# A two-layer decoder trunk on one core: a layer's last output products by column halves, and the pre-norm's second sum of squares on VectorE

## The chip, the cores and the metric

The kernel is one program on one core of a Trainium2 chip. The metric is device time in microseconds (us) from the first to the last work of one execution; every number is for that one core. The engines are TensorE (PE: matrix products and transposes, with PEld for its weight loads), VectorE (DVE), ScalarE (ACT), GpSimd (POOL), and SyncE (SP), whose queue starts all the DMA transfers. Each engine takes its instructions in a fixed order and waits on semaphores for the others.

## The reference

256 positions of 1024 channels go through two layers. Each layer has a token mixer (layer 0: native sparse attention; layer 1: a Mamba-2 scan) and then a gated ConvFFN. Each of these four sub-layers is wrapped in two norms:

```
def rms_norm(x, gain):
    y = xf * lax.rsqrt(jnp.mean(xf * xf, axis=-1, keepdims=True) + RMS_EPS)
    return (y * gain.astype(jnp.float32)).astype(x.dtype)
...
        hn = rms_norm(h, gains[0])
...
        h = h + rms_norm(m, gains[1])
        f = conv_ffn(rms_norm(h, gains[2]), ffn_w_up[i], ffn_conv_w[i], ffn_conv_b[i], ffn_w_down[i])
        h = h + rms_norm(f, gains[3])
```

So between two sub-layers the output of the first is normed and added to `h` (the post-norm), and the new `h` is normed for the next sub-layer (the pre-norm). Nothing in the next sub-layer can start before that.

## The kernel before

The stream `h` lies in SBUF as two tiles, `h0` and `h1`, of 128 positions by 1024 channels each; they are called token blocks 0 and 1 here. Every product is done in three passes (`mm3`), since both operands are split into a high and a low part: high by high, low by high, high by low. Weights come by DMA in pieces of 512 KB (`raw`); ACT casts each to its high part (`whi`, line 56), and DVE subtracts to get the low part (`wlo`, line 57). These two run all through the program, and the buffers of `raw`, `whi` and `wlo` are reused in turn (five of each in the common pool): a cast waits until PE has done with an older piece, and a load waits until DVE has done with an older `raw`.

A sub-layer ends in `out_mm`. It has a list of jobs (one for each 128 rows of the contraction) and two PSUM accumulators, one for each column half of 512 channels. It loops over the jobs and, inside, over the two halves. For the ConvFFN of layer 0 the last call has five jobs (the hidden pairs 17 to 21, whose `hm` tiles come from ACT and DVE), for that of layer 1 four; for the attention four; in the scan layer each group of heads is one call of four jobs. The call for token block 0 stands before that for token block 1.

Then, for each block, comes `after`: the post-norm (`postnorm`: ACT sums the squares of both halves, `junk` on line 126; POOL adds, `ms` on line 117, and takes the power -0.5, `rstd` on line 119; DVE multiplies by the gain, `fg` on line 161, and by `rstd` and adds to `h`, line 164), and the pre-norm (`prenorm_steps`: the same sum of squares on `h` through `rms`, then `xn` on DVE, line 146, eight transposes `pt` on PE, line 65, and the split into `xhi` on ACT and `xlo` on DVE). After the last sub-layer the post-norm alone follows, and then the stores. In the scan layer DVE first scales the accumulators into a tile `osb` (lines 812 and 814), and the post-norm reads that.

The order of instructions on each engine is not that of the source: a scheduler lays it out when the program is built, from its own estimates of when each result will be there. So a change in one place also moves other instructions nearby. The ConvFFN, the attention and the scan start their first product with token block 0 alone (`pv`), so that block 1's norm can run beside it.

Of the kernel before, what the change touches and what calls it, by code (L numbers as in the profile page):

```python
# [10 lines left out]
BF16 = mybir.dt.bfloat16  # L11
AF = mybir.ActivationFunctionType
OP = mybir.AluOpType
# [7 lines left out]
EPS = 1e-6  # L21
# [12 lines left out]
def trunk(ctx, tc, x, gains, consts, masks, params, nsa_in, nsa_vw, cmp_w1, nsa_out,  # L34
          ssd_in, ssd_dt, ssd_out, ffn_up, ffn_down, out):
    nc = tc.nc
# [3 lines left out]
    sp = ctx.enter_context(tc.tile_pool(name="sp", bufs=2))  # L40
# [8 lines left out]
    def tiny(shape, name):  # L49
        return sp.tile(shape, F32, name=name, tag="tiny", bufs=16)  # L50
# [16 lines left out]

    last_mm = [None]

    # weights: load, then split into two exact float32r parts; pieces of 4 KB a partition  # L70
    class Weights:
        def __init__(self, src, a, b, pool=None, n=5, order=(), first=nc.scalar.copy, into=None, lows=()):
            self.m, self.parts = min(a, 1024 // b), []
# [19 lines left out]
    weights = Weights  # L93
# [7 lines left out]
    mhalf = cp.tile([128, 1], F32, name="mhalf")  # L101
# [13 lines left out]
    def rstd_of(a, b, n):  # L115
        ms = tiny([128, n], "ms")
        nc.gpsimd.tensor_scalar(ms, a, b, EPS, op0=OP.mult if isinstance(b, float) else OP.add, op1=OP.add)  # L117
        r = tiny([128, n], "rstd")
        nc.gpsimd.tensor_tensor(r, ms, mhalf.to_broadcast([128, n]), op=OP.pow)
        return r  # L120

    def rms(src):
        ss = tiny([128, 2], "ss")
        for c in range(2):
            junk = sp.tile([128, 512], BF16, name="junk", tag="junk", bufs=2)
            nc.scalar.activation(junk, src[c], AF.Square, scale=1.0 / 32, accum_out=ss[:, c:c + 1])  # L126
        return rstd_of(ss[:, 0:1], ss[:, 1:2], 1)

    def new_xt():
        return (cp.tile([128, 2, KT, 128], F32R, name="xhi"), cp.tile([128, 2, KT, 128], F32R, name="xlo"))  # L130
# [8 lines left out]
        return marks  # L139

    def prenorm_steps(i, g, xt, pins):
        r = rms([h[i][:, :512], h[i][:, 512:]])
        xn = sp.tile([128, D], F32, name="xn", tag="xn", bufs=2)
        for c in range(2):
            cs = slice(512 * c, 512 * c + 512)
            z = nc.vector.scalar_tensor_tensor(xn[:, cs], h[i][:, cs], r, g[:, cs], op0=OP.mult, op1=OP.mult)
        yield [z.ins]
        for c in range(2):
            pt = pa([128, 4, 128], "pt")
            with after_ins(pins[c]):  # L150
                for k in range(4):
                    tr(pt[:, k, :], xn[:, 512 * c + 128 * k:512 * c + 128 * k + 128], ident)
            o = (slice(None), i, slice(4 * c, 4 * c + 4))
            yield [split(xt[0][o], xt[1][o], pt)]
# [11 lines left out]
    def mm3(o, ahi, alo, bhi, blo, first, last):  # L166
        mm(o, ahi, bhi, start=first, stop=False)
        mm(o, ahi, blo, start=False, stop=False)
        return mm(o, alo, bhi, start=False, stop=last)
# [41 lines left out]
    def out_mm(acc, i, jobs, first, last):  # L211
        marks = []
        ts = slice(128 * i, 128 * i + 128)
        for n, (a, ka, w, kw) in enumerate(jobs):
            for c in range(2):
                cs = slice(512 * c, 512 * c + 512)
                marks.append(mm3(acc[c], a[0][:, ka, ts], a[1][:, ka, ts], *w(kw, cs), first and n == 0,
                                 last and n == len(jobs) - 1).ins)
        return marks

    # ---------------------------------------------------------------- NSA
    def nsa(np_, xt, after):
        def one(shape, name, dt=F32):
            return np_.tile(shape, dt, name=name, bufs=1)
# [283 lines left out]
        after(0, accs[0], marks[-FN:][:2])  # L508
        after(1, accs[1])

    # ---------------------------------------------------------------- ConvFFN
    silu = [None]

    def tap0(c, ps, base, nt):
# [46 lines left out]
        after(0, accs[0], marks[-FA:][:2])  # L561
        after(1, accs[1])

    # ---------------------------------------------------------------- SSD
    def ssd(zp, yp, xt):
        def one(shape, name, dt=F32):
            return zp.tile(shape, dt, name=name, bufs=1)
# [248 lines left out]
                    after(i, [osb[:, i, :512], osb[:, i, 512:]], (None, None))  # L816
            todo = []

    # ---------------------------------------------------------------- trunk
    xt = new_xt()  # L820
    gain0 = load_gain(0)
    scaled, *marks0 = prenorm(0, gain0, xt)
# [161 lines left out]
```

## Time and profile before

| | |
|---|---|
| time before, median of 3 runs | 758.35 us (757.01 to 758.54) |
| span of the profiled execution, first to last instruction | 755.2 us (its own time is not given apart; the span lies 3.15 us under the median) |
| TensorE busy | 732.1 us (97% of the span) |
| VectorE busy | 570.3 us (76%) |
| ScalarE busy | 468.7 us (62%) |
| GpSimd busy | 65.6 us (9%) |

A busy share is an average over the program. With PE at 97%, what counts is where PE stands still (about 23 us in all, 6 of them after its last product), and which engine it waits for there.

### The profile page before, as it was taken

Reading aid. Unit: us, or ns where it says so; the run is one execution under the profiler, and the core shown is the slowest. Engines: PE = TensorE matmul, PEld = TensorE weight load, DVE = VectorE, ACT = ScalarE, POOL = GpSimd, SP = SyncE. Lnnn points to the kernel's source line nnn. Section 1 sums busy time; section 2 is a strip of 40 time slices with the busy share of each in tenths; the row PEclk is TensorE's granted clock in tenths of the full one; section 3 lists DMA queues with packets and bytes.
Section 4 is the critical chain, followed back from the end, with each engine's and each line's share of the span. In section 5 each row is a group of like instructions: output and inputs, shape, how many; then the busy total and the mean of one; then the engine's idle time right before and its main releaser. Section 6 shows DMA issues by size and latency. Waiting matters only on the chain.

```text
span 755.2 us, 13761 instructions
## 1 busy us (share of the span) xinstructions
PE 732.1 (97%) x5300; PEld 666.9 (88%) x5300; DVE 570.3 (76%) x927; ACT 468.7 (62%) x885; POOL 65.6 (9%) x95
## 2 busy tenths in 40 slices
PE   6989999999999999999999999999999999999996
PEld 4989877679999999997899998898778999999995
DVE  4687987747977767777698877679887967776783
ACT  5576768646655555565776686666566656555651
POOL 2310121211000000000000000024220000000000
PEclk9999999999999999999999999999999999999999
DMA  8864440315656555665355564125644665666531
GB/s 310 287 229 146 149 139 1 113 56 176 209 179 199 192 189 177 204 209 178 120 174 183 168 223 136 61 84 157 212 156 148 210 190 183 186 201 195 172 112 57
DMA packets 35427, 125.96 MB, mean 167 GB/s; under 512 B 4064, under 2 KB 4384, under 8 KB 35360
## 3 DMA queue, kind: packets, MB, share of 16 engines
q1 hardware_dynamic: 35360, 125.07, 51.1%
q8 instruction: 42, 0.69, 0.4%
q14 instruction: 25, 0.20, 0.1%
HBM read 124.00 MB, written 1.05 MB: 166 GB/s over the span
## 4 chain that ended last, share of the span: by engine, by line
PE 80%; DVE 9%; ACT 4%; DMA 3%; issue 2%; POOL 1%; SPq 0%; DVEq 0%; POOLq 0%; ACTq 0%
PE pu L61 44%; PE acc L61 18%; PE pv L61 5%; DVE wlo L57 4%; PE pt L65 3%; PE po L61 3%; PE sa L61 1%; ACT junk L126 1%; PE py L61 1%; ACT whi L56 1%; PE sb L61 1%; DMA gain<-in_gains 1%; PE pcx L61 1%; PE pc L61 1%; DMA raw<-in_ffn_down 1%
## 5 line engine op out<-in xcount | busy, mean ns | idle before, releaser
L57 DVE TENSOR_TENSOR wlo<-raw,whi 128x1024 fp32r<-128x1024 f32 (+1 forms) x220 | 268.3, 1226 | 81.1 <-ACT whi L56 80.5
L56 ACT CAST whi<-raw 128x1024 fp32r<-128x1024 f32 x223 | 231.1, 1045 | 106.9 <-PE pu L61 58.1
L61 PE MATMUL pu<-xhi,whi 128*128 128x256 f32 x1056 | 297.1, 281 | 0.1
L61 PE MATMUL pu<-xhi,wlo 128*128 128x256 f32 x1056 | 295.9, 281 | 0.0
L61 PE MATMUL pu<-xlo,whi 128*128 128x256 f32 x1056 | 295.4, 280 | 0.0
L61 PEld LDWEIGHTS pu<-xhi,whi 128*128 128x128 f32 x1056 | 199.1, 189 | 2.3 <-issue 0.5
L61 PEld LDWEIGHTS pu<-xlo,whi 128*128 128x128 f32 x1056 | 199.2, 189 | 1.2
L61 PEld LDWEIGHTS pu<-xhi,wlo 128*128 128x128 f32 x1056 | 199.0, 189 | 0.3 <-issue 0.2
L521 DVE SCALAR_TENSOR_TENSOR cc<-pu,pr,cc 128x255 f32<-128x255 f32 (+2 forms) x248 | 111.3, 477 | 6.8 <-ACT cc L515 3.7
L61 PE MATMUL acc<-whi,hm 128*128 128x512 f32 x352 | 114.6, 391 | 0.6 <-ACT hm L56 0.6
L61 PEld LDWEIGHTS acc<-whi,hm 128*128 128x128 f32 x352 | 66.1, 188 | 14.2 <-ACT hm L56 1.0
L61 PE MATMUL acc<-wlo,hm 128*128 128x512 f32 x176 | 69.0, 392 | 0.0
L515 ACT ACTIVATE cc<-pu,pr 128x256 f32<-128x256 f32 x112 | 57.8, 558 | 9.0 <-PE pu L61 8.8
L56 ACT CAST hm<-cc 128x256 fp32r<-128x256 f32 x44 | 17.8, 404 | 45.5 <-DVE cc L549 45.5
L117 POOL TENSOR_SCALAR ms<-ss 128x1 f32<-128x1 f32 x16 | 7.7, 479 | 420.5 <-ACT junk L126 420.5
L61 PE MATMUL acc<-whi,gw 128*128 128x512 f32 x128 | 41.3, 398 | 0.0
L61 PEld LDWEIGHTS acc<-wlo,hm 128*128 128x128 f32 x176 | 33.0, 188 | 5.6
L61 PE MATMUL pv<-whi,xhi 128*128 128x256 f32 (+1 forms) x128 | 36.4, 295 | 1.0 <-ACT whi L56 0.6
L61 PE MATMUL pv<-whi,xlo 128*128 128x256 f32 (+1 forms) x128 | 34.9, 288 | 1.0 <-DVE xlo L57 0.9
L61 PE MATMUL pv<-wlo,xhi 128*128 128x256 f32 (+1 forms) x128 | 35.2, 285 | 0.2 <-DVE wlo L57 0.2
L57 DVE TENSOR_TENSOR hm<-cc,hm 128x256 fp32r<-128x256 f32 x44 | 18.6, 423 | 14.6 <-ACT hm L56 14.6
L61 PEld LDWEIGHTS acc<-whi,gw 128*128 128x128 f32 x128 | 24.0, 188 | 5.2
(211 smaller groups left out, 896.4 us busy)
## 6 DMA issues: line engine op xcount, KB each, us to landing
raw<-in_ffn_up SPq DMA_DIRECT2D x88, 512.0 KB, 4.5
raw<-in_ffn_down SPq DMA_DIRECT2D x44, 512.0 KB, 4.7
raw<-in_ssd_in SPq DMA_DIRECT2D x40, 512.0 KB, 4.7
raw<-in_nsa_in SPq DMA_DIRECT2D x18, 512.0 KB, 5.0
raw<-in_ssd_out SPq DMA_DIRECT2D x16, 512.0 KB, 4.0
gain<-in_gains SPq DMA_DIRECT2D x8, 512.0 KB, 4.6
raw<-in_cmp_w SPq DMA_DIRECT2D x8, 512.0 KB, 5.4
raw<-in_nsa_out SPq DMA_DIRECT2D x8, 512.0 KB, 4.5
```

The costliest lines, as they stand in the source:

```text
L56: r = copy(hi, src)
L57: eng.tensor_tensor(lo, src, hi.bitcast(F32), op=OP.subtract)
L61: last_mm[0] = nc.tensor.matmul(*a, **k)
L65: last_mm[0] = nc.tensor.transpose(*a)
L117: nc.gpsimd.tensor_scalar(ms, a, b, EPS, op0=OP.mult if isinstance(b, float) else OP.add, op1=OP.add)
L126: nc.scalar.activation(junk, src[c], AF.Square, scale=1.0 / 32, accum_out=ss[:, c:c + 1])
L515: nc.scalar.activation(c, ps, AF.Identity, bias=pr[:, base + nt:base + nt + 1], scale=pr[:, base + nt - 1:base + nt])
L521: nc.vector.scalar_tensor_tensor(c[:, s:], ps[:, :S - s], wv, c[:, s:], op0=OP.mult, op1=OP.add)
```

## The change

It has two parts. In `out_mm`, a call that is the last one for its accumulators (`last`) now goes through all jobs for the first column half and then through all jobs for the second. In the pre-norm, `rms` is replaced by `rms_two`: ACT sums the squares of the first half only; POOL adds the epsilon to that sum; DVE multiplies the second half by itself and accumulates on top of POOL's result; POOL takes the power. The post-norm keeps `rms`. (Two comment lines are also gone.)

```
+    def square(src, out):
+        junk = sp.tile([128, 512], BF16, name="junk", tag="junk", bufs=2)
+        nc.scalar.activation(junk, src, AF.Square, scale=1.0 / 32, accum_out=out)
+
     def rms(src):
         ss = tiny([128, 2], "ss")
         for c in range(2):
-            junk = sp.tile([128, 512], BF16, name="junk", tag="junk", bufs=2)
-            nc.scalar.activation(junk, src[c], AF.Square, scale=1.0 / 32, accum_out=ss[:, c:c + 1])
+            square(src[c], ss[:, c:c + 1])
         return rstd_of(ss[:, 0:1], ss[:, 1:2], 1)
+
+    def rms_two(src):
+        ss, part = tiny([128, 2], "ss"), tiny([128, 1], "part")
+        square(src[0], ss[:, 0:1])
+        nc.gpsimd.tensor_scalar(part, ss[:, 0:1], EPS, None, op0=OP.add)
+        junk = sp.tile([128, 512], BF16, name="junk", tag="junk", bufs=2)
+        nc.vector.tensor_tensor_reduce(junk, src[1], src[1], 1.0 / 1024, part, OP.mult, OP.add, ss[:, 1:2])
+        r = tiny([128, 1], "rstd")
+        nc.gpsimd.tensor_tensor(r, ss[:, 1:2], mhalf, op=OP.pow)
+        return r
...
     def prenorm_steps(i, g, xt, pins):
-        r = rms([h[i][:, :512], h[i][:, 512:]])
+        r = rms_two([h[i][:, :512], h[i][:, 512:]])
...
     def out_mm(acc, i, jobs, first, last):
         marks = []
         ts = slice(128 * i, 128 * i + 128)
-        for n, (a, ka, w, kw) in enumerate(jobs):
-            for c in range(2):
-                cs = slice(512 * c, 512 * c + 512)
-                marks.append(mm3(acc[c], a[0][:, ka, ts], a[1][:, ka, ts], *w(kw, cs), first and n == 0,
-                                 last and n == len(jobs) - 1).ins)
+        steps = [(n, c) for n in range(len(jobs)) for c in range(2)]
+        if last:
+            steps.sort(key=lambda z: z[1])
+        for n, c in steps:
+            a, ka, w, kw = jobs[n]
+            cs = slice(512 * c, 512 * c + 512)
+            marks.append(mm3(acc[c], a[0][:, ka, ts], a[1][:, ka, ts], *w(kw, cs), first and n == 0,
+                             last and n == len(jobs) - 1).ins)
         return marks
```

In the built program the new sum is two instructions on DVE, both listed as `ISA`: the product with its accumulation, and a read of the accumulator into `ss`. There are eight of each, two for every sub-layer's pre-norm. Three places show how the order moved.

**TensorE, end of layer 0's ConvFFN, token block 0.** `acc_2519` and `acc_2520` are its two column halves; `hm_3600`, `hm_3697`, `hm_3782`, `hm_3879` and `hm_3964` are the hidden pairs 17 to 21. The run of 30 products begins with `hm_3600`. Before, the twelve that end the run:

```order
L61 MATMUL acc_2519<-whi_4005,hm_3879 128x512
L61 MATMUL acc_2519<-wlo_4006,hm_3879 128x512
L61 MATMUL acc_2519<-whi_4005,hm_3879 128x512
L61 MATMUL acc_2520<-whi_4005,hm_3879 128x512
L61 MATMUL acc_2520<-wlo_4006,hm_3879 128x512
L61 MATMUL acc_2520<-whi_4005,hm_3879 128x512
L61 MATMUL acc_2519<-whi_4011,hm_3964 128x512
L61 MATMUL acc_2519<-wlo_4012,hm_3964 128x512
L61 MATMUL acc_2519<-whi_4011,hm_3964 128x512
L61 MATMUL acc_2520<-whi_4011,hm_3964 128x512
L61 MATMUL acc_2520<-wlo_4012,hm_3964 128x512
L61 MATMUL acc_2520<-whi_4011,hm_3964 128x512
```

After, these are products 10 to 21 of the run:

```order
L61 MATMUL acc_2519<-whi_4005,hm_3879 128x512
L61 MATMUL acc_2519<-wlo_4006,hm_3879 128x512
L61 MATMUL acc_2519<-whi_4005,hm_3879 128x512
L61 MATMUL acc_2520<-whi_3975,hm_3600 128x512
L61 MATMUL acc_2520<-wlo_3976,hm_3600 128x512
L61 MATMUL acc_2520<-whi_3975,hm_3600 128x512
L61 MATMUL acc_2520<-whi_3993,hm_3697 128x512
L61 MATMUL acc_2519<-whi_4011,hm_3964 128x512
L61 MATMUL acc_2519<-wlo_4012,hm_3964 128x512
L61 MATMUL acc_2519<-whi_4011,hm_3964 128x512
L61 MATMUL acc_2520<-wlo_3994,hm_3697 128x512
L61 MATMUL acc_2520<-whi_3993,hm_3697 128x512
```

The first product with the last pair, `hm_3964`, stood behind 24 others and now stands behind 16; the scheduler put four products of the second half in front of it.

**VectorE, from layer 0's ConvFFN into the scan layer.** `acc_2521` and `acc_2522` are the halves of token block 1, `xlo` the split input of the next sub-layer for block 0, `wlo_4413` a piece of the scan's weights. Before:

```order
L164 SCALAR_TENSOR_TENSOR h0_70<-fg_4079,rstd_4087,h0_70 128x512 x2
L57 TENSOR_TENSOR wlo_4413<-raw_4410,whi_4412 128x1024
L146 SCALAR_TENSOR_TENSOR xn_4102<-h0_70,rstd_4100,gain_4077 128x512 x2
L161 TENSOR_TENSOR fg_4119<-acc_2521,gain_4075 128x512
L161 TENSOR_TENSOR fg_4119<-acc_2522,gain_4075 128x512
L57 TENSOR_TENSOR xlo_2031<-pt_4105,xhi_2030 128x512
L57 TENSOR_TENSOR xlo_2031<-pt_4112,xhi_2030 128x512
L164 SCALAR_TENSOR_TENSOR h1_71<-fg_4119,rstd_4127,h1_71 128x512 x2
```

After:

```order
L177 SCALAR_TENSOR_TENSOR h0_70<-fg_4079,rstd_4087,h0_70 128x512 x2
L137 ISA junk_4098,ss_4093<-h0_70,part_4094 128x512
L137 ISA ss_4093 128x1
L159 SCALAR_TENSOR_TENSOR xn_4102<-h0_70,rstd_4100,gain_4077 128x512 x2
L174 TENSOR_TENSOR fg_4119<-acc_2521,gain_4075 128x512
L57 TENSOR_TENSOR wlo_4413<-raw_4410,whi_4412 128x1024
L174 TENSOR_TENSOR fg_4119<-acc_2522,gain_4075 128x512
L57 TENSOR_TENSOR xlo_2031<-pt_4105,xhi_2030 128x512
L57 TENSOR_TENSOR xlo_2031<-pt_4112,xhi_2030 128x512
L177 SCALAR_TENSOR_TENSOR h1_71<-fg_4119,rstd_4127,h1_71 128x512 x2
```

The weight's `wlo_4413` stood ahead of block 0's `xn`; it now stands between the two `fg` of block 1, ahead of both `xlo`.

**VectorE, from the scan layer into layer 1's ConvFFN, token block 1.** `acc_6489` and `acc_6490` are the halves of block 1's last accumulators; `wlo_6563`, `wlo_6569` and `wlo_6731` are pieces of the ConvFFN's weights, the first two those of its second `pv`. Before:

```order
L57 TENSOR_TENSOR wlo_6563<-raw_6560,whi_6562 128x1024
L57 TENSOR_TENSOR xlo_4147<-pt_6454,xhi_4146 128x512
L57 TENSOR_TENSOR wlo_6569<-raw_6566,whi_6568 128x1024
L814 SCALAR_TENSOR_TENSOR osb_6052<-acc_6489,rstd_6413,osb_6052 128x512
L814 SCALAR_TENSOR_TENSOR osb_6052<-acc_6490,rstd_6413,osb_6052 128x512
L161 TENSOR_TENSOR fg_6517<-osb_6052,gain_6417 128x512 x2
L164 SCALAR_TENSOR_TENSOR h1_71<-fg_6517,rstd_6525,h1_71 128x512 x2
L57 TENSOR_TENSOR wlo_6731<-raw_6728,whi_6730 128x1024
L146 SCALAR_TENSOR_TENSOR xn_6540<-h1_71,rstd_6538,gain_6419 128x512 x2
```

After:

```order
L174 TENSOR_TENSOR fg_6517<-osb_6052,gain_6417 128x512
L830 SCALAR_TENSOR_TENSOR osb_6052<-acc_6490,rstd_6413,osb_6052 128x512
L57 TENSOR_TENSOR wlo_6563<-raw_6560,whi_6562 128x1024
L174 TENSOR_TENSOR fg_6517<-osb_6052,gain_6417 128x512
L177 SCALAR_TENSOR_TENSOR h1_71<-fg_6517,rstd_6525,h1_71 128x512 x2
L57 TENSOR_TENSOR wlo_6569<-raw_6566,whi_6568 128x1024
L137 ISA junk_6536,ss_6531<-h1_71,part_6532 128x512
L137 ISA ss_6531 128x1
L57 TENSOR_TENSOR wlo_6731<-raw_6728,whi_6730 128x1024
L159 SCALAR_TENSOR_TENSOR xn_6540<-h1_71,rstd_6538,gain_6419 128x512 x2
```

`wlo_6569` moved from the front of block 1's post-norm to behind its `h1`, ahead of the new sum, and `wlo_6731` now stands between the new sum and the `xn` that needs POOL's power of it.

## Rows read from the trace of the kernel before

**Rows 1.** The page's head: span, then busy time of each engine.

```profile
span 755.2 us, 13761 instructions
...
PE 732.1 (97%) x5300; PEld 666.9 (88%) x5300; DVE 570.3 (76%) x927; ACT 468.7 (62%) x885; POOL 65.6 (9%) x95
```

**Rows 2.** The tile `xn`: ns minimum/median/maximum; who waited, us and times.

```profile
L146 DVE SCALAR_TENSOR_TENSOR xn<-h,rstd,gain x16: 743/749/753, 9.4 to 568.2; 128x512 f32<-128x512 f32 x16
...
PE pt L65: 7.5, 5
```

**Rows 3.** The line 126, squares of one half: the square, the accumulator's read.

```profile
L126 ACT ACTIVATE junk<-h x16: 615/631/632, 3.8 to 565.6; 128x512 bf16<-128x512 f32 x16
L126 ACT ACTIVATION_READ_ACCUMULATOR junk<-h x16: 185/187/189, 4.4 to 566.2; 128x1 f32 x16
```

**Rows 4.** Timeline, end of layer 0's ConvFFN: start, us, instruction, idle before.

```profile
340.88 0.39 PE L61 MATMUL acc<-whi,hm 128*128 128x512 f32 x1
...
348.84 0.39 PE L61 MATMUL acc<-whi,hm 128*128 128x512 f32 x1
349.39 0.40 ACT L56 CAST hm<-cc 128x256 fp32r<-128x256 f32 x1 [1.82 <-DVE cc L549]
349.85 0.50 PE L61 MATMUL acc<-whi,hm 128*128 128x512 f32 x1 [0.62 <-ACT hm L56]
...
352.90 1.06 ACT L56 CAST whi<-raw 128x1024 fp32r<-128x1024 f32 x1 [0.67 <-PE acc L61]
```

**Rows 5.** Timeline, from layer 0's ConvFFN into the scan layer.

```profile
358.46 1.35 DVE L161 TENSOR_TENSOR fg<-acc,gain 128x512 f32<-128x512 f32 x2 [0.35 <-ACT junk L126]
359.73 1.28 DVE L57 TENSOR_TENSOR xlo<-pt,xhi 128x512 fp32r<-128x512 f32 x2
...
360.46 0.39 PE L61 MATMUL pv<-whi,xlo 128*128 128x256 f32 x1
```

**Rows 6.** Timeline, attention into ConvFFN, token block 0's pre-norm.

```profile
165.30 0.63 ACT L126 ACTIVATE junk<-h 128x512 bf16<-128x512 f32 x1 [1.92 <-DVE h L164]
...
166.78 0.30 POOL L117 TENSOR_SCALAR ms<-ss 128x1 f32<-128x1 f32 x1 [2.37 <-ACT junk L126]
...
167.17 0.56 POOL L119 TENSOR_TENSOR rstd<-ms,mhalf 128x1 f32<-128x1 f32 x1
...
168.67 1.29 PE L65 MATMUL pt<-ident,xn 128*128 128x128 f32 x8 [0.58 <-DVE xn L146]
```

**Rows 7.** Timeline, the same place, token block 1.

```profile
172.63 1.40 DVE L164 SCALAR_TENSOR_TENSOR h<-fg,rstd,h 128x512 f32<-128x512 f32 x2
...
173.95 1.22 DVE L57 TENSOR_TENSOR wlo<-raw,whi 128x1024 fp32r<-128x1024 f32 x1
...
176.91 1.29 PE L65 MATMUL pt<-ident,xn 128*128 128x128 f32 x8
```

**Rows 8.** Timeline of VectorE and of GpSimd, out of the scan layer.

```profile
551.49 2.35 DVE L57 TENSOR_TENSOR wlo<-raw,whi 128x1024 fp32r<-128x1024 f32 x2
...
552.54 1.39 POOL L117 TENSOR_SCALAR ms<-ss 128x1 f32<-128x1 f32 x1 [2.42 <-ACT junk L126]
```

**Rows 9.** Timeline, out of the scan layer: TensorE's two waits, block 1's `h`.

```profile
555.51 0.63 PE L65 MATMUL pt<-ident,xn 128*128 128x128 f32 x4 [1.48 <-DVE xn L146]
...
564.17 1.41 DVE L164 SCALAR_TENSOR_TENSOR h<-fg,rstd,h 128x512 f32<-128x512 f32 x2 [0.84 <-POOL rstd L119]
...
568.37 0.66 PE L65 MATMUL pt<-ident,xn 128*128 128x128 f32 x4 [1.53 <-DVE xn L146]
```

**Rows 10.** Waits of ScalarE, 505 to 562 us: total, times, longest.

```profile
ACT whi L56 <- PE acc L61: 1.8, 5, 0.4
```

**Rows 11.** Timeline, start of the program, token block 1's transposes.

```profile
16.93 0.63 PE L65 MATMUL pt<-ident,xn 128*128 128x128 f32 x4 [0.65 <-DVE xn L146]
```

**Rows 12.** Timeline, the last product and the last square.

```profile
748.51 0.39 PE L61 MATMUL acc<-whi,hm 128*128 128x512 f32 x1
...
748.99 0.60 ACT L126 ACTIVATE junk<-acc 128x512 bf16<-128x512 f32 x1
```

## The prediction

> **What bounds the kernel now.** The page comes first: PE is busy in 97% of the span [rows 1]. So an edit counts only where PE stands still, or comes to. The view of the tile `xn` says who makes it stand at the norms: 7.5 us in 5 waits for `xn` [rows 2]. Then the timeline of each passage between two sub-layers is read for what ends the wait. Out of the attention PE waits 0.58 us for block 0 and nothing for block 1 [rows 6, 7]; out of the scan it waits 1.48 and 1.53 us [rows 9]; at the start 0.65 us [rows 11]. Out of layer 0's ConvFFN it waits before the norm, 0.62 us for the last `hm` [rows 4].
>
> **What the change costs, part by part.**
>
> *The column halves and the squares.* One could expect the first half's square to move under the second half's products, and a square to vanish from the path. The end of the program shows that it was under them already: PE starts the last product at 748.51 and ends it at 748.90, and ACT starts the second half's square at 748.99 [rows 12]. Three products, the lead that a half has in the old order, last 0.68 us; a square of 0.63 [rows 3] fits in that. What is left to gain is the 0.09 us between the two, say 0.05. The end term is -0.05.
>
> *The last `hm`.* The new order asks for each job's operands earlier. In rows 4 thirty-six products start from 340.88 to 348.84, the last 24 of them being the first 24 of the run: (348.84 - 340.88)/35 = 0.227 us each. The run thus begins at 340.88 + 12 x 0.227 = 343.61, and the first product with `hm_3964` was due at 349.07; it started at 349.85, since ACT began that `hm` at 349.39 [rows 4]. The built order puts it behind 16 products instead of 24, so PE is there at 343.61 + 16 x 0.227 = 347.25. ACT and DVE get `hm` ready by work that the change does not touch, so PE stands for 2.60 us instead of 0.78: **+1.82**, eight products that used to cover the wait. They follow after it, when nothing waits for them. It is zero only if `hm` comes 1.8 us earlier; nothing can make it more, since behind 349.85 the two orders have the same products.
>
> *A weight ahead of `xlo`.* The cast at 352.90 waited for PE to give back a piece of down weights [rows 4]. That is the piece of pair 17; its last use was the sixth product of block 1's run and is now the eighteenth. The cast and its `wlo` slide, and the built order has the `wlo` between the two `fg`, ahead of `xlo`. Before, DVE waited 0.35 us ahead of the first `fg`, did two `fg` and two `xlo`, and PE took the first `xlo` at 360.46, 0.05 after its end [rows 5]. A `wlo` takes 1.22 [rows 7]. DVE, no longer idle, saves about 0.25 of it; `xlo` and with it PE comes 0.97 later. Bounds 0 (it slips in earlier) and 1.2. I take **+0.95**. The new sums here cost nothing: block 0's `xn` is ready about 0.5 us before PE has finished block 1's run; if that cover went, 0.3 us would show.
>
> *The new sum, by itself.* The old path from the first square to the power is 167.17 - 165.30 = 1.87 us [rows 6]. The new one is: square and read 0.69 (two of them and a hop of 0.1 take 166.78 - 165.30 = 1.48), a hop of 0.1 to POOL, 0.30 there, 0.04 to DVE, the sum, its read, a hop of 0.1. No row shows the new instruction. From below it is a square's step of 0.63; the nearest row is `xn`, DVE's other operation on 512 fp32 elements with two SBUF tensors, at 0.75 [rows 2]; from above it is 1.28, `xn` plus another 512 elements at a cycle each (2 x 0.64, a pair's span of 1.28 in rows 5). For its read I take ACT's 0.19 [rows 3]. The sum is 0.69 + 0.1 + 0.30 + 0.04 + 0.75 + 0.19 + 0.1 = 2.17, so each pre-norm is **0.3 longer**, not shorter, with bounds 0.2 and 0.85. The second square gone from ACT buys nothing: ACT is busy 62% [rows 1].
>
> [...]
>
> *The new sum in its queues.* It also makes DVE and POOL wait for each other, and POOL waits for DVE's `wlo`: `ms`, normally 0.30 [rows 6], took 1.39 while two `wlo` ran from 551.49 to 553.84, and ended 0.09 behind them [rows 8]. [...] The old path gave POOL two operations in a row; the new one has DVE between them, and the scheduler has put a `wlo` into the gap in places.
> - Attention into ConvFFN: block 0's transposes are 0.3 later. Block 1's `h` follows at about 173.0 and the `wlo` behind it, shifted with it, ends at 175.55 [rows 7]. POOL's first operation waits for it, to 175.75; sum and read to 176.7; the power to 177.4; `xn` 0.75 more; transposes at 178.3 instead of 176.91 [rows 7], where PE did not wait before. **+1.4** in all (bounds 0.3, if only block 0's part shows, and 2.4, with two sums of 1.28).
> - Out of the scan, block 0's wait falls from 1.48 to about 0.75, for the built order puts eight more products in front of its transposes (8 x 0.23 = 1.9 against an `xn` that is 0.3 to 1.2 later). Block 1's `h` can so start at 563.25 instead of 564.17 [rows 9]. But `wlo_6569` now stands behind it, 564.55 to 565.75. The sum follows until 566.95; `wlo_6731` until 568.1, with POOL's power locked out; 0.56 for the power [rows 6], 0.75 for `xn`. Transposes at 569.5 instead of 568.37 [rows 9]: **+1.2** (bounds -1.1, the first wait's gain kept and more, and +2.3). The second `pv` needs `wlo_6569` as well, and its stall lies inside this.
> - Start: the same pattern, a `wlo` between the sum and `xn` of block 1. Its wait of 0.65 [rows 11] grows to about 1.2: **+0.55** (0 to 1.1).
>
> In the scan's output phase the four jobs' weights are wanted earlier as well, but the scheduler interleaves the halves there, and each `wlo` comes as PE reaches it; zero, with 0.5 either way.
>
> **The sum**: -0.05 + 1.82 + 0.95 + 1.4 + 1.2 + 0.55 = +5.9 us on the span of 755.2. The span lies 3.15 under the median of the runs; on the median it gives 758.35 + 5.9 = **764.2 us**. With all lower bounds together (`hm` stays) it is 758.35 + 1.0 = 759.3, with all upper ones and the 0.5 of the output phase 767.7.
>
> **The rivals.**
> - *Sums at double length.* The 1.28 for 0.75 adds 0.53 wherever a sum is exposed: at the start, twice out of the attention, once into the scan, twice out of it. 6 x 0.53 = 3.2 more: 767.4 us. [...]
> - *The output phase of the scan takes up the lateness.* If DVE's casts and scalings from 505 to 562 us ran at their own pace, PE's lateness of 4.7 by then would eat into the waits of 1.48 and 1.53 and the scan would end as before, less what the halves give: accumulators that are half done 2 us earlier, and both waits gone. That is faster: 758.35 - 3.0 = 755.3 us at the best. It decides where DVE's chain there does not wait for PE. Against it: ACT's casts in that stretch waited for PE five times [rows 10], and DVE's `wlo` wait for those casts, so the lateness is handed on.
> - *Half of that*, the lateness eaten by the waits but no gain left: 4.7 - 3.0 = 1.7 of lateness, less than 1 us of which the halves return: 758.5 to 759.5 us, no change.
> - *The change does not do what it says.* Where the scheduler interleaves the halves again, as in the built order of the scan's middle groups, the halves are as before and only the sums remain: 0.55 + 1.4 + 1.2 = 3.2, 761.5 us. For the ConvFFN the built order excludes it; this lies inside the forecast's range.
>
> **How the numbers follow.** A measurement of this kernel can tell about 0.2%, 1.5 us. Forecast, 759.9 to 767: 0.60, its likeliest 764.2. Doubled sums, 767 and above: 0.12. No change, 756.8 to 759.9: 0.15. Faster: 0.13. The range leaves out most of the faster case and the end of the slow one: 757 to 768. Slower by over 0.2% is 0.60 + 0.12 = 0.72.
>
> **What the changed profile would show.** PE's wait for the last `hm` of layer 0 near 2.4 us (right) or 0.6 (wrong). `xlo` into the scan behind a `wlo` and PE waiting about 1 us for it. The new sum on DVE at 0.75 and its read near 0.2. POOL's operations of the pre-norm over 1 us wherever a `wlo` runs. Out of the scan a first wait under 1 us and a second above 1.5 us, or a stall in the second `pv` ahead of it. The end: the last square 0.04 instead of 0.09 behind the last product. What would make the prediction wrong is above all an earlier `hm`, or a scan whose end does not feel that its start was late.

## The result, and the profile after

The changed kernel takes 762.55 us (median of 4 runs, 760.3 to 763.11) against 757.68 for the kernel before (4 runs, 755.85 to 758.54): ratio 1.0066, 95% interval 1.0051 to 1.0081. It is slower by 5.0 us where 5.9 was forecast; 764.2 was too much by 1.7, and 0.7 of that is the kernel before, whose median fell from 758.35 to 757.68 with the fourth run. The profiled execution, the fastest of the four (760.3), has a span of 758.5 us, 1.8 under its time. With the same difference the profiled execution of before, whose span is 755.2, took about 757.0. The two spans differ by 3.3 us; the rest of the 5.0 is taken up with the halves alone, below.

The page's head shows PE as busy as before, and the time as added standing [rows 1]:

```profile
span 758.5 us, 13752 instructions
...
PE 731.8 (96%) x5300; PEld 665.9 (88%) x5300; DVE 575.8 (76%) x943; ACT 463.8 (61%) x869; POOL 66.8 (9%) x95
```

The new sum in the views of the tiles `part` and `ss` (ns minimum/median/maximum). The sum takes 752 ns, what `xn` takes (749 [rows 2]), not twice that, and its read 84, half of ACT's 187 [rows 3]. POOL's two operations have maxima of 1.10 and 1.47 us beside medians of 0.22 and 0.57; below it is seen where.

```profile
L135 POOL TENSOR_SCALAR part<-ss x8: 221/222/1101, 4.8 to 567.5; 128x1 f32<-128x1 f32 x8
L137 DVE CUSTOM_DVE_ANT_0 junk<-h,part x8: 749/752/753, 5.1 to 568.5; 128x512 bf16<-128x512 f32 x8
```

```profile
L137 DVE DVE_READ_ACCUMULATOR2_ANT ss<- x8: 82/84/86, 5.7 to 569.2; 128x1 f32 x8
L139 POOL TENSOR_TENSOR rstd<-ss,mhalf x8: 559/566/1471, 5.9 to 569.4; 128x1 f32<-128x1 f32 x8
```

The timeline at the end of layer 0's ConvFFN answers to [rows 4]. `hm` is ready 0.3 us earlier than before, as is the whole program there, but PE wants it eight products sooner and stands for 2.48 us instead of 0.62:

```profile
343.44 1.05 ACT L56 CAST whi<-raw 128x1024 fp32r<-128x1024 f32 x1 [0.54 <-PE acc L61]
344.40 1.01 ACT L531 ACTIVATE cc<-pu,pr 128x256 f32<-128x256 f32 x2
...
349.07 0.41 ACT L56 CAST hm<-cc 128x256 fp32r<-128x256 f32 x1 [1.90 <-DVE cc L565]
349.53 0.50 PE L61 MATMUL acc<-whi,hm 128*128 128x512 f32 x1 [2.48 <-ACT hm L56]
```

Into the scan [rows 5], a `wlo` stands between the two `fg`, `xlo` starts 2.13 us later, and PE waits 0.77 us for it, where rows 5 list no wait:

```profile
359.52 0.68 DVE L174 TENSOR_TENSOR fg<-acc,gain 128x512 f32<-128x512 f32 x1
...
360.12 1.21 DVE L57 TENSOR_TENSOR wlo<-raw,whi 128x1024 fp32r<-128x1024 f32 x1
...
361.86 1.28 DVE L57 TENSOR_TENSOR xlo<-pt,xhi 128x512 fp32r<-128x512 f32 x2
362.59 0.39 PE L61 MATMUL pv<-whi,xlo 128*128 128x256 f32 x1 [0.77 <-DVE xlo L57]
```

Out of the attention [rows 6, 7]. Block 0's transposes come 1.11 us earlier than before and block 1's only 0.39, so this passage costs 0.72. In block 0 VectorE has finished `h` at 163.30 + 1.42 = 164.72 and then waits 0.51 us for POOL's `part` before it starts its sum. In block 1 `part` takes 0.97 and ends at 174.15, 0.09 behind the `wlo`:

```profile
163.30 1.42 DVE L177 SCALAR_TENSOR_TENSOR h<-fg,rstd,h 128x512 f32<-128x512 f32 x2 [0.35 <-POOL rstd L119]
164.14 0.63 ACT L124 ACTIVATE junk<-h 128x512 bf16<-128x512 f32 x1 [1.92 <-DVE h L177]
...
164.96 0.22 POOL L135 TENSOR_SCALAR part<-ss 128x1 f32<-128x1 f32 x1 [1.70 <-ACT junk L124]
165.22 0.75 DVE L137 CUSTOM_DVE_ANT_0 junk<-h,part 128x512 bf16<-128x512 f32 x1 [0.51 <-POOL part L135]
...
165.89 0.09 DVE L137 DVE_READ_ACCUMULATOR2_ANT ss<- 128x1 f32 x1
166.06 0.56 POOL L139 TENSOR_TENSOR rstd<-ss,mhalf 128x1 f32<-128x1 f32 x1 [0.88 <-DVE ss L137]
...
167.56 1.29 PE L65 MATMUL pt<-ident,xn 128*128 128x128 f32 x8 [0.63 <-DVE xn L159]
...
172.84 1.22 DVE L57 TENSOR_TENSOR wlo<-raw,whi 128x1024 fp32r<-128x1024 f32 x1
...
173.18 0.97 POOL L135 TENSOR_SCALAR part<-ss 128x1 f32<-128x1 f32 x1 [4.20 <-ACT junk L124]
...
176.52 0.63 PE L65 MATMUL pt<-ident,xn 128*128 128x128 f32 x4 [0.48 <-DVE xn L159]
```

Out of the scan [rows 8, 9] the two waits of 1.48 and 1.53 us have become four: 0.64, 1.56 for a `wlo` that stands behind block 1's `h`, 0.46 and 0.76. The power took 1.47 us, against its median of 0.57, where it started during a `wlo`:

```profile
558.50 1.29 PE L65 MATMUL pt<-ident,xn 128*128 128x128 f32 x8 [0.64 <-DVE xn L159]
...
561.92 0.40 PE L61 MATMUL acc<-whi,gw 128*128 128x512 f32 x1
...
568.47 0.39 PE L61 MATMUL pv<-wlo,xhi 128*128 128x256 f32 x1 [1.56 <-DVE wlo L57]
...
569.20 1.22 DVE L57 TENSOR_TENSOR wlo<-raw,whi 128x1024 fp32r<-128x1024 f32 x1
569.37 1.47 POOL L139 TENSOR_TENSOR rstd<-ss,mhalf 128x1 f32<-128x1 f32 x1 [0.88 <-DVE ss L137]
...
570.49 0.44 PE L65 MATMUL pu<-ident,ut 128*128 128x128 f32 x2 [0.46 <-ACT ut L194]
...
571.68 1.32 PE L65 MATMUL pt<-ident,xn 128*128 128x128 f32 x8 [0.76 <-DVE xn L159]
```

The line at 561.92 is the last of the scan's output products. In the kernel before it started 1.38 us earlier:

```profile
560.54 0.40 PE L61 MATMUL acc<-whi,gw 128*128 128x512 f32 x1
```

### The profile page after: what moved, and what is told of

It reads as the page before. It is cut to its first block, busy times and chain, and to the rows that moved or that the text cites. A ratio compares the mean times of both kernels' runs of the same rounds, so it can differ in the third digit from the quotient of the medians.

```text
span 758.5 us, 13752 instructions
## 1 busy us (share of the span) xinstructions
PE 731.8 (96%) x5300; PEld 665.9 (88%) x5300; DVE 575.8 (76%) x943; ACT 463.8 (61%) x869; POOL 66.8 (9%) x95
## 4 chain that ended last, share of the span: by engine, by line
PE 82%; DVE 7%; ACT 4%; issue 2%; DMA 2%; POOL 2%; SPq 0%; DVEq 0%; POOLq 0%; ACTq 0%
PE pu L61 46%; PE acc L61 20%; PE pv L61 4%; PE pt L65 3%; PE po L61 3%; DVE wlo L57 2%; PE py L61 1%; PE sa L61 1%; PE sb L61 1%; PE pcx L61 1%; ACT whi L56 1%; DMA gain<-in_gains 1%; ACT junk L124 1%; DMA raw<-in_ssd_out 1%; ACT P L404 1%
## 5 line engine op out<-in xcount | busy, mean ns | idle before, releaser
L117 POOL TENSOR_SCALAR ms<-ss 128x1 f32<-128x1 f32 x8 | 3.9, 488 | 393.6 <-ACT junk L124 393.6
```

## Experiments

Twelve kernels, each timed in five rounds beside the kernel before. 0.001 of the ratio is 0.76 us.

**Sums alone.** The changed kernel without the sort:

```diff
-        if last:
-            steps.sort(key=lambda z: z[1])
```

> The pre-norm's squares are shared between ScalarE and VectorE as in the changed kernel; the last output products go job by job, as in the kernel before. My theory: the two parts of the change add. The order's share is the stall on the last `hm` (2.48 against 0.62 us) and `xlo` behind a `wlo` (0.8), 2.7 us; the sums' share is what is left of the 4.9 us by which the medians differ, about +2.2 us on the kernel before. PE's wait for the last `hm` is 0.6 us again, PE waits about 0.5 us for block 1's transposes out of the attention, and POOL's `part` takes about 1 us wherever a `wlo` runs. Rival A: the sums cost nothing, since their path is only 0.05 us longer where nothing locks POOL: within 0.5 us of the kernel before. Rival B: the parts do not add, and the sums alone cost 4 us or more.

Measured: 759.45 us, ratio 1.0027 (1.0014 to 1.0039), +2.0 us: about the 2.2 of the forecast, and both rivals fall. But the wait for `hm` was not 0.6 in its trace: 1.84, in the old order. The timeline shows why: ACT's two casts ahead of `cc` waited 1.71 and 0.92 us for the DMA of the scan's weights. So the amount alone does not say that the sums cost it; the sums with an earlier `hm`, below, do.

```profile
343.83 1.05 ACT L56 CAST whi<-raw 128x1024 fp32r<-128x1024 f32 x1 [1.71 <-DMA raw<-in_ssd_in]
...
345.80 1.06 ACT L56 CAST whi<-raw 128x1024 fp32r<-128x1024 f32 x1 [0.92 <-DMA raw<-in_ssd_in]
...
351.89 0.50 PE L61 MATMUL acc<-whi,hm 128*128 128x512 f32 x1 [1.84 <-ACT hm L56]
```

**Halves alone.** The old squares in the pre-norm:

```diff
-        r = rms_two([h[i][:, :512], h[i][:, 512:]])
+        r = rms([h[i][:, :512], h[i][:, 512:]])
```

> The last output products go by column halves as in the changed kernel; the pre-norm's two squares are both on ScalarE, as before. My theory: the stall on the last `hm` of layer 0's ConvFFN (1.9) and the `wlo` ahead of `xlo` into the scan (0.8) stand in this kernel unchanged, 2.7 us; out of the scan the halves give back some of it, for eight more products stand ahead of block 0's transposes and the old squares follow at once: between +1.5 and +2.7 us on the kernel before. Rival A: the losses come from the sums, and the halves are hidden or gain: 0 or faster. Rival B: the scan's output phase hands the lateness on in full and the halves add waits of their own there: +4 us.

Measured: 761.08 us, ratio 1.0052 (1.0034 to 1.0070), +3.9 us, more than my range and near rival B's amount. The waits that rival B adds in the scan's output phase are not there: the trace is 2.17 us late at the first `xlo` product into the scan and 1.86 at the program's last product. The two stalls are there (2.52 for `hm`, 0.64 for `xlo`), and something else: from the wait's end to the first product into the scan PE takes 13.2 us, where the changed kernel takes 361.08 - 349.53 = 11.55 for the same products:

```profile
348.04 0.50 PE L61 MATMUL acc<-whi,hm 128*128 128x512 f32 x1 [2.52 <-ACT hm L56]
...
361.25 0.39 PE L61 MATMUL pv<-whi,xhi 128*128 128x256 f32 x1 [0.44 <-ACT xhi L56]
```

The view of windows (busy time of each engine, then PE's granted clock as a fraction of full speed) shows the 1.7 us: behind the wait the clock fell, to 0.64 and 0.94 in the two windows.

```profile
348.00:352.00 4.00, 3.96 (x11) 3.08 (x12) 1.12 (x2) 0.69 (x2) 0.00 (x0) 0.64 0.54 185
352.00:356.00 4.00, 4.00 (x18) 3.26 (x17) 1.77 (x3) 0.92 (x3) 0.86 (x2) 0.94 0.00 0
```

(1 - 0.64) x 4 + (1 - 0.94) x 4 = 1.7. The span of this execution, the fastest of the six, is only 1.9 us above that of before, since it was ahead until then: out of the attention its block 0 transposes came at 166.73, 1.94 us earlier than before [rows 6]. From there to the last product it loses 3.8, which agrees with the +3.9. The changed kernel's trace was 1.11 ahead at that place, and its clock is 1.00 in both windows: two reasons why its span is only 3.3 above that of before and its median 5.0.

**Job-by-job order in layer 0's ConvFFN alone**, halves elsewhere:

```diff
-        if last:
+        if last and halves:
             steps.sort(key=lambda z: z[1])
...
-            return out_mm(accs[i], i, [(hs[p], 0, wd[p // 2], p % 2) for p in ps], ps[0] == 0, ps[-1] == NP - 1)
+            return out_mm(accs[i], i, [(hs[p], 0, wd[p // 2], p % 2) for p in ps], ps[0] == 0, ps[-1] == NP - 1, l == 1)
```

> The changed kernel, with job-by-job order again in layer 0's ConvFFN alone; halves elsewhere. My theory: the stall on the last `hm` falls from 2.48 to 0.6 us and the `wlo` leaves the place ahead of `xlo`, so that 2.7 us of the 4.9 come back: about +2.2 us on the kernel before (ratio 1.003). Rival A: the scan's output phase takes up the lateness of the ConvFFN, so it did not reach the end: within 0.7 us of the changed kernel (ratio 1.006). Rival B: halves in layer 0's ConvFFN are the whole loss: no slower than the kernel before.

Measured: 760.52 us, ratio 1.0037 (1.0022 to 1.0052), +2.8 us where my theory had +2.2: 2.2 come back instead of 2.7, and the lateness from there does reach the end. The wait for `hm` is 1.08.

**The two sums side by side.**

```diff
-        nc.gpsimd.tensor_scalar(part, ss[:, 0:1], EPS, None, op0=OP.add)
...
-        nc.vector.tensor_tensor_reduce(junk, src[1], src[1], 1.0 / 1024, part, OP.mult, OP.add, ss[:, 1:2])
-        r = tiny([128, 1], "rstd")
-        nc.gpsimd.tensor_tensor(r, ss[:, 1:2], mhalf, op=OP.pow)
-        return r
+        nc.vector.tensor_tensor_reduce(junk, src[1], src[1], 1.0 / 1024, 0.0, OP.mult, OP.add, ss[:, 1:2])
+        return rstd_of(ss[:, 0:1], ss[:, 1:2], 1)
```

> The changed kernel, but VectorE's sum starts from zero instead of from ScalarE's sum, and GpSimd adds the two and the epsilon and then takes the power, as before: the two halves are summed side by side. My theory: the path from the first square to the power is shorter by the smaller of the two, 0.6 to 0.7 us, and VectorE waits for GpSimd no more; that counts where PE stands for `xn` (the start, out of the attention and out of the scan, each for one or both blocks), 3 to 4 us less than the changed kernel: +1 to +2 us on the kernel before (ratio 1.001 to 1.003). Rival: where a `wlo` is running GpSimd is locked out either way and the end of the lock decides, so that the shorter path is lost and the time stays within 1 us of the changed kernel (ratio 1.005 or more).

Measured: 763.65 us, ratio 1.0095 (1.0075 to 1.0115): no gain at all, and my picture of the path falls with it. The timeline out of the attention, block 0:

```profile
165.08 1.42 DVE L174 SCALAR_TENSOR_TENSOR h<-fg,rstd,h 128x512 f32<-128x512 f32 x2 [0.35 <-POOL rstd L119]
165.93 0.63 ACT L124 ACTIVATE junk<-h 128x512 bf16<-128x512 f32 x1 [1.93 <-DVE h L174]
...
166.53 0.69 DVE L136 CUSTOM_DVE_ANT_0 junk<-h 128x512 bf16<-128x512 f32 x1
...
167.40 0.30 POOL L117 TENSOR_SCALAR ms<-ss 128x1 f32<-128x1 f32 x1 [2.35 <-ACT junk L124]
167.78 0.57 POOL L119 TENSOR_TENSOR rstd<-ms,mhalf 128x1 f32<-128x1 f32 x1
```

VectorE makes the second half of `h` while ScalarE squares the first, so its sum cannot start before 166.53, 0.60 behind the square's start; chained to `part` it started 165.22 - 164.14 = 1.08 behind it. (165.22 is the changed kernel's sum, 164.14 its square, both shown above.) That is 0.48 gained, and POOL's additional operation takes 0.38 of it back. From the start of `h` to the end of the power it is 3.27 us here and 3.32 there. What this kernel lost beyond the changed one is not settled in full; in its trace, of the slowest of six executions (767.46), the wait for `hm` was 3.29, and the clock fell behind it (0.72 and 0.85 in the windows from 352 to 360 us) and again out of the scan (0.50 from 576 to 580).

**An earlier `hm`.** The casts of the scan's first weights go behind the last `hm`:

```diff
-                split(hm[:, 0, 0], hm[:, 1, 0], cc[:, 0, :])
+                late_hm[0] = split(hm[:, 0, 0], hm[:, 1, 0], cc[:, 0, :])
...
-        ws = [weights(ssd_in[16 + u], KT, 256) for u in range(SFILL)]
+        ws = [weights(ssd_in[16 + u], KT, 256, order=[late_hm[0]] * 2) for u in range(SFILL)]
```

> The changed kernel, with ScalarE's casts of the scan's first weights (`in_ssd_in`) put behind the last `hm` of layer 0's ConvFFN; before, two of them stood ahead of its `cc` and waited for their DMA. My theory: the last `hm` was late because of these casts: the last `pu` product ended at 340.79 and `cc` began only at 344.40, behind casts at 341.85 and 343.44. Without them, and without the `wlo` of 1.22 between the taps and the multiply, `hm` comes at about 344.7, ahead of the 347.05 at which PE wants it in the new order; PE's wait of 2.48 us is gone, and with it a fall of the granted clock behind it, which cost 1.6 us in two of the three traces with halves there. So 2.5 to 3.5 us less than the changed kernel, +1 to +2.5 us on the kernel before (ratio 1.0015 to 1.003). Rival: the casts and their `wlo` come into the way of the post-norm's squares and `fg` instead, and the time stays within 1 us of the changed kernel (ratio 1.005 to 1.007).

Measured: 759.14 us, ratio 1.0018 (1.0008 to 1.0029): 3.6 us of the 5.0 come back. `cc` starts at 341.25 and `hm` is there at 345.2; PE does not wait for it.

```profile
341.25 1.02 ACT L531 ACTIVATE cc<-pu,pr 128x256 f32<-128x256 f32 x2
...
344.77 0.41 ACT L56 CAST hm<-cc 128x256 fp32r<-128x256 f32 x1 [0.96 <-DVE cc L565]
345.08 2.95 ACT L56 CAST whi<-raw 128x1024 fp32r<-128x1024 f32 x3
```

**PE kept busy through the wait.** The changed kernel with eleven products more, whose result is not used:

```diff
...
+            if fill and n == len(jobs) - 1 and c == 0:
+                pw2 = pa([128, 512], "pw")
+                with tc.issue_after(marks[-1]):
+                    for d in range(11):
+                        pin = mm(pw2, jobs[0][0][0][:, jobs[0][1], ts], jobs[0][2](jobs[0][3], cs)[0], start=True, stop=True).ins
+            with after_ins(pin):
+                marks.append(mm3(acc[c], a[0][:, ka, ts], a[1][:, ka, ts], *w(kw, cs), first and n == 0,
+                                 last and n == len(jobs) - 1).ins)
...
```

> The changed kernel, with 11 products more of 0.227 us each, on operands that are there already and into a scratch PSUM tile, right ahead of the first product that waits for the last `hm` of layer 0's ConvFFN: PE works through the wait of 2.48 us instead of standing. Nothing else moves. My theory: standing for 2.5 us and more lets the granted clock fall to its lower level behind the wait in most executions (0.64 from 348 to 352 us in the halves-only trace, 0.72 in that with the sums side by side), which costs about 1.6 us each time. With PE busy the clock stays at 1.0 from 346 to 360 us and the median is about 1 us below the changed kernel's: +3.5 to +4 us on the kernel before (ratio 1.005). Rival: the clock has nothing to do with this wait; the median is the changed kernel's (1.0066), or above it by what the 11 products overshoot.

Measured: 762.82 us, ratio 1.0068 (1.0053 to 1.0083), the rival's figure. It does not settle the clock, though: the eleven products did not cover the wait. A cast had waited 1.53 us for its DMA, `hm` came 4.60 us after PE wanted it (2.65 of filling, 1.95 of standing), and behind the 1.95 the clock fell all the same, to 0.86 and 0.72 in the two windows from 348 to 356.

```profile
344.64 1.05 ACT L56 CAST whi<-raw 128x1024 fp32r<-128x1024 f32 x1 [1.53 <-DMA raw<-in_ssd_in]
...
346.13 2.65 PE L61 MATMUL pw<-whi,hm 128*128 128x512 f32 x11
...
350.73 0.71 PE L61 MATMUL acc<-whi,hm 128*128 128x512 f32 x1 [1.95 <-ACT hm L56]
```

**The earlier `hm` in the kernel before**, by the same edit.

> The kernel before, with the same casts behind the last `hm` and nothing else. My theory: its wait of 0.62 us for `hm` is gone (in other executions of the old order it was 1.1 and 1.8), so 0.6 to 1.2 us less: ratio 0.9985. Rival: the four `wlo` of 1.22 us that then stand ahead of the post-norm's first `fg` reach past the end of block 0's products and delay the pre-norm: 0 to +1 us.

Measured: 756.18 us, ratio 0.9980 (0.9970 to 0.9989): faster than the kernel before by 1.5 us, somewhat more than the 0.6 to 1.2 I gave. The first `fg` of the norm starts at 350.90 there, 0.66 earlier than before, so the `wlo` do not delay it.

**Halves in the scan's output products alone**, all else as before:

```diff
...
-        if last:
+        if halves:
             steps.sort(key=lambda z: z[1])
...
-                    marks = out_mm(acc, i, jobs, True, True)
+                    marks = out_mm(acc, i, jobs, True, True, True)
```

> The kernel before, with column halves in the scan's output products alone; both ConvFFN and the attention job by job, both squares on ScalarE. My theory: halves cost only where the last operand is late. In the scan's output phase, the halves-only trace stood 2.17 us behind the trace of before at the first `xlo` product into the scan and about 1.5 at the transposes of block 1 out of it, so they give back 0.6 us there: ratio 0.999, on the edge of what can be told. Rival: that gain was only the lateness eaten up by waits that the kernel before has anyway (1.48 and 1.53 us), and alone the halves give nothing or cost up to 1 us.

Measured: 757.11 us, ratio 0.9991 (0.9980 to 1.0002): the forecast figure, but the interval holds 1, so a gain there is not shown.

**The parts without the wait for `hm`.** The sums, and the halves, each with the early `hm` edit.

> The kernel before with the early `hm` (its casts behind the last `hm`, ratio 0.998 alone), and the new sums; products job by job. It measures the sums without the wait for `hm`, which in the sums-only trace was 1.84 us against 0.62. My theory: the sums cost what the traces show at the norms, about 0.6 us for block 1 out of the attention, 0.4 more in sum out of the scan, and little at the start, where the transposes stood about 0.5 us later relative to the first ones: +1 us on the early `hm` alone, ratio 0.9990 to 1.0000. Rival: the 2 us of the sums-only kernel were the sums' own: ratio 1.0007 or more.

> The changed kernel's column halves everywhere and both squares on ScalarE, with the early `hm`. My theory: without the wait for `hm` the halves cost 0.8 us for `xlo` behind a `wlo` into the scan and give back about 0.6 out of it: ratio 0.998 to 0.9985, level with the early `hm` alone, against 1.0052 for the halves without it. Rival: part of the halves' cost is elsewhere, and the ratio is 1.000 or more.

Measured: sums 757.84 us, ratio 1.0006 (0.9995 to 1.0017); halves 756.29 us, ratio 0.9982 (0.9973 to 0.9991). Once `hm` is early the halves alone cost nothing that shows (0.0002, with intervals of 0.001 either way). The sums cost 0.0026 more than the early `hm` alone, 2.0 us as without it: this falls between my theory and the rival, and nearer the rival, since the sums' price has nothing to do with `hm`. Where it arises shows beside the trace of the early `hm` alone: the sums' trace is 0.46 us ahead at block 0's transposes out of the attention (168.04 against 168.50), 0.26 behind at the first of layer 0's last `hm` products (341.00 against 340.74), 0.60 behind at the first of the scan's output products (510.89 against 510.29) and 1.19 at the program's last product (748.86 against 747.67). So 0.72 come out of the attention, 0.34 into the scan and 0.59 out of it, 1.7 in all.

**`xlo` ahead of the `wlo`.** The whole change with the early `hm`, and the casts of the scan's third weight tile (both pieces) put behind block 0's `xhi`:

```diff
+                    late_x[0] = list(steps)[-1][0]
...
-                ps = pair(weights(ssd_in[16 + u], KT, 256), xt, True)
+                ps = pair(weights(ssd_in[16 + u], KT, 256, order=[late_x[0]] * 2 if u == SFILL else ()), xt, True)
```

> The whole change with the early `hm` (ratio 1.0018), and the cast of the first piece of the scan's third weight tile put behind block 0's `xhi`, so that no `wlo` stands between the two `fg` ahead of `xlo` into the scan. My theory: PE's wait of 0.77 us for `xlo` there falls to 0.1 or so, and the span by 0.8 us: ratio 1.0006 to 1.0010. Rival: the `wlo` only moves, and delays block 1's sum and `xn` instead; no gain, ratio 1.0018 or more.

Measured: 758.08 us, ratio 1.0006 (0.9997 to 1.0015) against 1.0018. PE's wait for `xlo` is gone from the trace, and the 0.9 us agree with its 0.77; the two intervals overlap, so the size rests on the trace.

**The best of these parts together**: the kernel before, with the early `hm` and halves in the scan's output alone.

> The kernel before with the early `hm` (ratio 0.998) and column halves in the scan's output products alone (0.9991). My theory: the two lie 200 us apart and add: ratio 0.997, the fastest of all these kernels. Rival: the lead of 1.4 us that the early `hm` gives is eaten in the scan's output phase once the halves are there, and it is no faster than the early `hm` alone.

Measured: 755.57 us, ratio 0.9981 (0.9971 to 0.9991): faster than the kernel before by 1.4 us, and not to be told from the early `hm` alone. That is the rival's outcome. That anything eats a second gain is not shown: the trace of the scan's halves alone starts its last product at 748.47 against 748.51 before [rows 12], so there may have been none.

## Why the prediction was right, step by step

The four kernels with and without each part, and the same with the early `hm`, as ratios to the kernel before:

| | neither part | sums | halves | both |
|---|---|---|---|---|
| `hm` behind the casts | 1 | 1.0027 | 1.0052 | 1.0066 |
| `hm` ahead of them | 0.9980 | 1.0006 | 0.9982 | 1.0018 |

- **The last `hm`, +1.82.** Right in mechanism, and 1.86 in the profiled execution. It was mis-sized for the others. The step "ACT and DVE get `hm` ready by work that the change does not touch" took `hm`'s time as one number. It hangs on the casts ahead of it in ACT's queue, most of which waited for a DMA (in the changed kernel's trace the last of them waited 0.54 us for PE), and varies: the old order waited 0.62, 1.84, 1.08 and 0.61 us in four traces (mean 1.04), the halves 2.48, 2.52, 3.29 and, with the eleven products in it, 4.60 (mean 3.2). That is 2.2 more, and in three of these four the clock fell behind the wait, 1.7 us each, while it fell in none of the first four: 3.5 us together. By the table the halves cost 0.0052 and 0.0039 with the late `hm`, 0.0002 and 0.0012 with the early one: 2.1 to 3.8 us hang on this one wait, against the 1.82 I gave it. So "nothing can make it more" failed as well.
- **A `wlo` ahead of `xlo`, +0.95.** Right: 0.77 in the trace, and gone with the cast moved.
- **The sums, +3.15 in all** (0.55, 1.4 and 1.2). The sign is right and the size too large: 2.0 us in two of the four comparisons in the table (0.0027 and 0.0026), 1.1 and 2.7 in the others (0.0014 and 0.0036). What failed is "each pre-norm is 0.3 longer". From the first square to the power it is 166.06 - 164.14 = 1.92 us against 1.87 before. The sum starts 1.08 behind the square where I had 1.13, the read 0.67 behind the sum's start instead of 0.75, and the power 0.17 behind the read's instead of 0.29, for the read that I took at 0.19 takes 0.084. What remains is the queue: out of the attention 0.72 instead of 1.4, all of it in block 1 behind a `wlo`. "The new sums here cost nothing", said of the way into the scan, failed too: 0.34 there in the pair of traces above.
- **Out of the scan, +1.2.** Right in size and in mechanism. The lateness is 2.13 us at `xlo`'s product, 3.31 at block 1's transposes and 3.3 at the end, so 1.2 in all. Block 0's transposes start 2.99 later, but eight more products (1.8 us) stand in front of them. The last of the output products is only 1.38 late, since PE's first wait fell from 1.48 to 0.64 (I had 0.75). Between there and block 1's transposes 1.93 are lost: the stall in the second `pv` is there as given, 1.56, and the wait for `ut` is one that I did not have.
- **The start, +0.55.** Not there; this step failed. Block 0's transposes came at 9.14 instead of 10.18, since the gains landed earlier (the first `xn`, which waited for them, started at 8.33 instead of 9.38); in the fourteen traces that time lies between 8.86 and 10.30, with either part or none. PE's wait of 0.65 for block 1's `xn` [rows 11] did not grow to 1.2: in the changed kernel the transposes start at 17.96 without a wait, and in no trace with the new sums does PE wait longer than 0.34 for them. Relative to block 0's transposes the program is 0.57 later at the attention's first `pht` product (41.38 us behind them against 40.81), but there PE's clock was lower, as the lines below show. From block 0's transposes to that product it is 41.2 us in the mean of the six traces with the old sums, and 41.2 in that of the eight with the new.
- **The end, -0.05.** Nothing: the last square starts 0.09 behind the last product's end, as before [rows 12].
- **Doubled sums**, the strongest rival on the slow side, fall: 0.752 us beside `xn`'s 0.749. Their 1.28 was my estimate, and no run shows the cycle it counts in; what the trace of before shows for another 512 elements is 0.53 us (products of two SBUF tensors: 0.69 for `xe`, 128x512, and 1.22 for `xs`, 128x1024), and the new sum does not take it.
- **The output phase takes up the lateness** falls too: restoring the order in layer 0's ConvFFN gave 2.2 us at the end, and an early `hm` 3.6.

That the whole came within 0.9 us of the 5.9 is partly luck: the sums were 1.1 too large in it, and the halves, 2.77 with `hm` and `xlo`, measured 3.0 and 3.9 in the table, an error the other way.

The lines for the start are block 1's transposes in the changed kernel, and the windows from 12 to 16 us of the kernel before and of the changed one, with PE's clock at 0.84 and 0.50:

```profile
17.96 0.60 PE L65 MATMUL pt<-ident,xn 128*128 128x128 f32 x4
```

```profile
12.00:16.00 4.00, 3.43 (x23) 3.13 (x23) 2.98 (x4) 3.81 (x8) 0.86 (x2) 0.84 1.03 415
```

```profile
12.00:16.00 4.00, 3.86 (x18) 3.86 (x19) 3.72 (x6) 3.31 (x6) 2.20 (x2) 0.50 1.03 415
```

The clock is shown as a companion of these waits, not as their proven consequence: the kernel that was to keep PE busy did not keep it busy long enough. It also bears on the sums: out of the scan, PE waits for `wlo`, `ut` and `xn` in close order, and among these or right behind them the clock fell in three traces with the new sums (lowest window 0.60 with the sums alone, 0.50 with the sums side by side and in the last but one kernel). From 564 to 576 us it stayed at 1.00 in the changed kernel and, with the old sums, in the kernel before, in the halves with and without the early `hm`, and in the last kernel. The windows of the last but one:

```profile
564.00:568.00 4.00, 1.98 (x15) 1.65 (x13) 3.51 (x5) 0.94 (x3) 2.46 (x2) 0.95 0.79 280
568.00:572.00 4.00, 3.50 (x16) 2.89 (x15) 2.59 (x4) 1.17 (x2) 0.04 (x1) 0.50 0.49 167
572.00:576.00 4.00, 4.00 (x26) 4.00 (x26) 1.04 (x2) 1.32 (x3) 0.00 (x0) 0.69 0.01 2
```

(0.05 + 0.50 + 0.31) x 4 = 3.4 us of clock. Three traces are too few to give this a share of the 2.0 us; that stays open.

## What to carry to other kernels

An order that asks for each operand earlier spends the products that covered the last one: count them, and look at what stands ahead of that operand in its engine's queue, for here two casts of weights that nobody needed yet, waiting for a DMA, held it up, and moving them alone won 1.5 us. Two halves of a sum on two engines saved next to nothing here, where the second engine was still making the data (3.27 us against 3.32); and a hop to GpSimd that fell into a `wlo` of VectorE ended behind it: 0.97 us instead of 0.22 and 1.47 instead of 0.57, beside a `wlo`'s 1.22. One profiled execution gives one draw of a wait that hangs on a DMA (0.61 to 1.84 us in four traces of the old order): take the same wait from several before it becomes a term.

## What the runs showed of the hardware

- The sum of products over 512 fp32 elements with a running start took 752 ns on VectorE, as long as an operation without a sum (`xn`, 749 [rows 2]), and its read of the accumulator 84 ns against ScalarE's 187 [rows 3].
- PE's granted clock fell behind waits of some 2 us in some executions and not in others: 1.00 behind 2.48 us of standing, 0.64 behind 2.52 (windows of 4 us), and a fall to 0.86 and 0.72 behind 1.95 that followed 2.65 us of products. At the attention's wait near 57 us it fell behind 1.67 us in the kernel before (0.70 and 0.87 in the windows from 56 to 64) and stayed at 1.00 behind 2.39 in the last but one kernel. The falls at layer 0's `hm` cost 1.7 us each, nearly as much as the eight products did.
- Of the sixteen [128 x 1] operations of POOL in the changed kernel's pre-norms, the five that started during a `wlo` took 0.97 to 1.10 us (`part`) and 1.37 to 1.47 (the power), against 0.22 and 0.57. Those `part` ended 0.08 or 0.09 us behind the `wlo`, those powers 0.42 and 0.44. This is what the runs show of the "locked out" in the prediction and the expectations; what holds POOL back they do not show. A post-norm's power that started at 168.41, 0.18 ahead of a `wlo`, kept its 0.57.
